# Hybrid decoder layer: first modulation rows loaded ahead of three pieces of the token-major x, idle matmuls behind the spread of the root mean square, row constants loaded later

## The chip, the cores and the metric

The kernel runs on one core of one Trainium2 chip. The metric is the device time of one execution in microseconds (us), smaller is better. Before the change the median of three runs is 734.33 us (732.56 to 735.61).

## The reference

One layer on x of 512 tokens by 2048 features, all float32:

```python
mod = silu(c) @ w_ada + b_ada                 # 3 * 2048
shift, scale, gate = split(mod, 3)
h = rms_norm(x) * (1.0 + scale) + shift
proj = h @ w_in                               # 4160 columns
xr, gr, qc, kvc, kr, ga = split(proj)
y_rnn = rg_lru_branch(xr, ...) * silu(gr)
y_att = mla_branch(qc, kvc, kr, positions, ...) * silu(ga)
x = x + gate * (concat([y_rnn, y_att]) @ w_out)
```

rms_norm divides each token by the root of the mean of its squares over the 2048 features, so it needs every feature of x before the first h can be made.

## The kernel before

**Layout.** Features lie on the 128 partitions and the 512 tokens along the free dimension: x, h and the projections are tiles of 128x512. The 2048 features are 16 tiles k. The projection goes over k in four chunks (`CHUNKS`: 2, 3, 4 and 7 tiles). Each product in float32 is made of three matmuls on split operands (high times high, high times low, low times high): ScalarE rounds the high part (`whi`, `wfs` half 0, `h`), VectorE subtracts for the low part (`wlo`, `wfs` half 1).

**The modulation.** Row j of the modulation is 128 values, the sums of w_ada times silu(c). `ada(j, parts)` (line 280) loads a 128x2048 piece of w_ada in the given parts (a part of 2 is 128x1024, 512 KB) and has VectorE multiply and sum each part (`ttr`, line 273; the operation stands in the profile as CUSTOM_DVE_ANT_0 at L276). `ada(16 + k)` gives the scale of tile k, `ada(k)` its shift. They share three buffers. `cb` holds silu(c) on every partition, made by eight matmuls and four copies.

**The start.** The token-major x (`xtok`) comes in eight pieces of 128x1024, 512 KB each (`xsq`, line 369; here called pieces 0 to 7). ScalarE squares and sums each one (`sqj`, sums in `ss8`). For every even piece TensorE transposes the first two feature tiles into `xps`, which ScalarE copies to `x0` and `x1`. Once all eight sums are there, VectorE and ScalarE make the inverse root mean square `rx` (lines 409 to 415), four matmuls spread it over the partitions (`rb_ps`, line 418), and VectorE makes tile 0: `x0` times scale and `rb_ps` (line 433), plus shift (line 442), the low part (line 445). Tile 1 follows with its own scale and shift. `proj_first` (line 497) then does the first eight column tiles with h0 (24 matmuls) and h1 (24 matmuls) and the weights `wfs`.

**Idle matmuls.** `warm(n, after)` (line 246) issues matmuls of a tile of ones (`junk`) into a bank that nobody reads: 4 at the start, 6 after each squared piece, 4 after the reciprocal, 14 behind the spread in program order. "After" is an order that is asked of the scheduler, not a wait on the chip.

**What sets the order.** SyncE's queue issues nearly all transfers in program order. The other engines' orders are set by a scheduler that simulates a timeline; each engine then runs its list in that order. `behind()` and `issue_after` tell it that an instruction may not stand before another. The vector constants (`vec`) and the first scale row `ada(16)` are loaded when the loop over the pieces reaches number `XA`, here 7. The row constants (`row`, a part for the attention's gains and one for its mask, and `pos_i`, the positions) are loaded behind the first weights (lines 463 to 465); VectorE scales and casts them as part of `setup_rope` (line 290).

```python
        if n == XA:
            DMA.dma_start(out=vec, in_=a["vec"])
            ts(vec[:, 16:32], vec[:, 16:32], 1.0, None, ALU.add)
            run(ada0[0])
        xsq(n // 2, n % 2)
```

Of the kernel before, what the change touches and what calls it, by code (L numbers as in the profile page):

```python
# [20 lines left out]
P = 128  # L21
# [17 lines left out]
NB0 = 0  # L39
NB1 = 1  # L40
P0 = 8
XA = 7
SETUP = (0, 2)
WARM = (4, 6, 4, 14)
NACC = 6
GRATE = 1.1
BANKS = dict(u=(0, 1), f=(2,), sc=(4, 5), tp=(6,), op=(6,), tq=(7,), oa=(2, 3, 0, 1, 7, 4, 5, 6))
# [4 lines left out]
R_QN, R_KN, R_QR, R_KR, R_IF, R_ID, R_MK, NROW = 0, 128, 256, 320, 384, 416, 544, 672  # L52
# [32 lines left out]
def body(ctx, nc, tc, a):  # L85
    V, G, A, PE, DMA = nc.vector, nc.gpsimd, nc.scalar, nc.tensor, nc.sync
    last_tab = [None]

    def act(out, in_, func, **kw):
        return A.activation(out=out, in_=in_, func=func, **kw)  # L90

    def tab(out, in_, func, **kw):
        if last_tab[0] is None:
            i = act(out, in_, func, **kw)
        else:
            with tc.issue_after(last_tab[0]):
                i = act(out, in_, func, **kw)
        last_tab[0] = i.ins if hasattr(i, "ins") else i
        return i

    def stt(out, in0, scalar, in1, op0, op1, **kw):
        return V.scalar_tensor_tensor(out=out, in0=in0, scalar=scalar, in1=in1, op0=op0, op1=op1, **kw)
# [6 lines left out]
    def ins_of(i):  # L109
        return i.ins if hasattr(i, "ins") else i  # L110

    def ts(o, i, s1, s2, o0, o1=None):
        if s2 is None:
            return V.tensor_scalar(out=o, in0=i, scalar1=s1, scalar2=None, op0=o0)
        return V.tensor_scalar(out=o, in0=i, scalar1=s1, scalar2=s2, op0=o0, op1=o1)
# [6 lines left out]
        return tt(lo, src, hi.bitcast(F32), ALU.subtract)  # L122

    def mm(out, lhsT, rhs, start, stop, **kw):
        PE.matmul(out=out, lhsT=lhsT, rhs=rhs, start=start, stop=stop, **kw)  # L125

    def mm3(out, wh, wl, xh, xl, start, stop, **kw):
        mm(out, wh, xh, start, False, **kw)
# [3 lines left out]
    def cols(i):  # L132
        return slice(i * P, (i + 1) * P)
# [14 lines left out]
    def run(gen):  # L148
        for _ in gen:
            pass  # L150
# [18 lines left out]
    def bank(kind, name):  # L169
        return psp.tile([P, S], F32, tag=f"b{next(cyc[kind])}", name=name)  # L170
# [6 lines left out]
    def bigt(n, name, dt=F32):  # L177
        return big.tile([P, 2, S], dt, tag=f"B{n}", name=name)
# [24 lines left out]
    row = cst.tile([P, NROW], F32, name="row")  # L203
    pos_i = cst.tile([P, NT], I32, name="pos_i")
    ident = row[:, R_ID:R_ID + P]
# [37 lines left out]
    def warm(n, after=None):  # L243
        with tc.issue_after(ins_of(after)) if after is not None else nullcontext():
            for _ in range(n):
                mm(junk_ps, junk[:, :P], junk, True, True)

    warm(WARM[0])
    cps = [bank("mm", "cb_ps") for _ in range(4)]
# [17 lines left out]
    def xload(k, keep=False):  # L267
        xt[k] = pjt(34 + k, F32, f"x{k}") if keep else xslot(f"x{k}")
        DMA.dma_start(out=xt[k], in_=a["x"][k])
# [4 lines left out]
    def ttr(t, cv, j, first, last):  # L274
        with behind():
            ttr_last[0] = V.tensor_tensor_reduce(  # L276
                out=t, in0=t, in1=cv, op0=ALU.mult, op1=ALU.add, scale=1.0,
                scalar=vec[:, C_BADA + j:C_BADA + j + 1] if first else modh[:, j:j + 1],
                accum_out=(mod if last else modh)[:, j:j + 1])

    def ada(j, parts=(4,)):
        t = p1.tile([P, 4, S], F32, tag="ada", name="ada", bufs=3)
        n0 = 0
        for w in parts:
            c = slice(n0, n0 + w)
            DMA.dma_start(out=t[:, c], in_=a["ada"][j][:, n0 * S:(n0 + w) * S].rearrange("p (k s) -> p k s", k=w))
            ttr(t[:, c], cb[:, c], j, n0 == 0, n0 + w == 4)
            n0 += w
            yield
# [79 lines left out]
    def xsq(i, j):  # L369
        t = bigt((2, 3, 8, 9, 10, 11, 12, 13)[2 * i + j], "xtok").rearrange("p k s -> p (k s)")  # L370
        DMA.dma_start(out=t, in_=a["xtok"][i][:, j * 1024:(j + 1) * 1024])
        sq = act(sqj, t, AF.Square, accum_out=ss8[:, j * 4 + i:j * 4 + i + 1])
        if j == 0:
            for k in range(KT0):
                PE.transpose(xps[k][:, i * P:(i + 1) * P], t[:, k * P:(k + 1) * P], ident)
        warm(WARM[1], sq)

    hh, hl = {}, {}
    ada0 = [ada(16, (2, 2)), ada(0, (2, 1, 1))]
    KT0 = CHUNKS[0][1]  # L380
    NG = NF // 4
    wfs = {(k, n): bigt(4 + k * NG + n, "wfs", F32R) for k in range(KT0) for n in range(NG)}
# [2 lines left out]
    def wf_load(k, n):  # L385
        raw = wfraw[k, n]
        DMA.dma_start(out=raw, in_=a["winf"][k, n])
        act(wfs[k, n][:, 0], raw, AF.Copy)

    def wf_lo(k, n):  # L390
        tt(wfs[k, n][:, 1], wfraw[k, n], wfs[k, n][:, 0].bitcast(F32), ALU.subtract)
# [3 lines left out]
    for n in range(2 * NT):  # L395
        if n == XA:
            DMA.dma_start(out=vec, in_=a["vec"])
            ts(vec[:, 16:32], vec[:, 16:32], 1.0, None, ALU.add)
            run(ada0[0])
        xsq(n // 2, n % 2)  # L400
    wf_load(0, 0)
    tab(p1.tile([P, 1], F32, name="sqrt0"), ones[:, 0:1], AF.Sqrt)
# [5 lines left out]
    vx, yx, tx, rx = (p1.tile([P, NT], F32, name=n) for n in ("vx", "yx", "tx", "rx"))  # L408
    tt(vx, ss8[:, 0:4], ss8[:, 4:8], ALU.add)
    ts(vx, vx, 1.0 / D, EPS, ALU.mult, ALU.add)  # L410
    warm(WARM[2], V.reciprocal(out=tx, in_=vx))
    tab(yx, tx, AF.Sqrt)
# [2 lines left out]
    mark[0] = ins_of(stt(rx, tx, 1.5, yx, ALU.add, ALU.mult))  # L415
    rb_ps = bank("aux", "rb_ps")
    for i in range(NT):
        mm(rb_ps[:, cols(i)], rx[:, i:i + 1].broadcast_to([P, P]), ident, True, True)
    rb = p1.tile([P, S], F32, tag="rb", name="rb")
    warm(WARM[3])  # L420

    def make_h(k):
        if k >= KT0:
            xload(k)
        parts = (2, 2) if k < KT0 else (4,)
        if k:
            yield from ada(16 + k, parts)
        x = xt[k]
        if k == 0:
            next(ada0[1])  # L430
            next(ada0[1])
            stt(x, x, mod[:, 16:17], rb_ps, ALU.mult, ALU.mult)
            act(rb, rb_ps, AF.Copy)
            yield from ada0[1]
        else:
            yield from ada(k, parts)
            stt(x, x, mod[:, 16 + k:17 + k], rb, ALU.mult, ALU.mult)
        t = bigt(k, f"h{k}", F32R)
        hh[k], hl[k] = t[:, 0], t[:, 1]
        if k < KT0:  # L440
            ts(hh[k], x, mod[:, k:k + 1], None, ALU.add)
        else:
            act(hh[k], x, AF.Identity, bias=mod[:, k:k + 1])
        i = stt(hl[k], x, mod[:, k:k + 1], hh[k].bitcast(F32), ALU.add, ALU.subtract)
        if k < KT0:
            mark[0] = ins_of(i)
# [12 lines left out]
    for n in range(NG):  # L459
        wf_load(1, n)  # L460
        with behind():
            wf_lo(1, n)
    DMA.dma_start(out=row[:, :R_ID], in_=a["row"][:, :R_ID])
    DMA.dma_start(out=row[:, R_MK:], in_=a["row"][:, R_MK:])
    DMA.dma_start(out=pos_i, in_=a["pos"])


    XR, GR, QC, KVC, GA, KR = 0, 8, 16, 20, 24, 32
# [34 lines left out]
    def proj_first(ms):  # L503
        k0, kc = CHUNKS[0]
        ps = [bank("mm" if n < 6 else "aux", "pp") for n, m in enumerate(ms)]
        for k in range(k0, k0 + kc):
            for i, (w, h) in enumerate(((0, hh), (0, hl), (1, hh))):
                for n, m in enumerate(ms):
                    mm(ps[n], wfs[k, n // 4][:, w, (n % 4) * P:(n % 4 + 1) * P], h[k], k == k0 and i == 0, k == k0 + kc - 1 and i == 2)
        for n, m in enumerate(ms):  # L510
            evac(0, m, ps[n])

    def proj_kr(ci):
        k0, kc = CHUNKS[ci]
        ps = bank("mm", "pk")
        raw = wraw()
        DMA.dma_start(out=raw[:, :kc * 64], in_=a[f"wkr{ci}"])
        hl_ = wtile("whi", "wkhl")
        w3 = hl_[:, :kc * P].rearrange("p (k h c) -> p k h c", k=kc, h=2)
        r3 = raw[:, :kc * 64].rearrange("p (k c) -> p k c", k=kc)  # L520
        act(w3[:, :, 0], r3, AF.Copy)
        tt(w3[:, :, 1], r3, w3[:, :, 0].bitcast(F32), ALU.subtract)
        for i, (h, l) in enumerate(hs(ci)):
            mm(ps, hl_[:, cols(i)], h, i == 0, False)
            mm(ps, hl_[:, cols(i)], l, False, i == kc - 1)
        evac(ci, KR, ps)

    LC = NCH - 1
    for ci in range(LC):
        nk0, nkc = CHUNKS[ci + 1]  # L530
        hgen = itertools.chain.from_iterable(make_h(k) for k in range(nk0, nk0 + nkc))
        done = 0
        ng = 32 // GROUP[ci]
        g0 = NF // GROUP[ci] if ci == 0 else 0
        if ci == 0:
            proj_first(MORDER[:NF])
        for g in range(g0, ng):
            while done < 2 * nkc * (g + 1 - g0) // (ng - 1 - g0):
                next(hgen, None)
                done += 1  # L540
            if g == (g0 + ng) // 2:
                proj_kr(ci)
            proj_group(ci, g)
        run(hgen)
    p1ctx.close()
    extra_raw[0] = False

# [641 lines left out]
```

## Time and profile before

| | |
|---|---|
| median of three runs | 734.33 us (732.56 to 735.61) |
| the profiled execution | 734.08 us |
| its span | 732.3 us |
| TensorE matmul busy | 720.5 us (98%) |
| TensorE weight load busy | 597.4 us (82%) |
| VectorE busy | 527.1 us (72%) |
| ScalarE busy | 353.6 us (48%) |
| mean granted TensorE clock | 0.995 of full |
| moved by the DMA engines | 127.94 MB, mean 175 GB/s |

Between the span and the time of the execution lie 1.8 us. A matmul's busy time in the profile includes its latency, so matmuls overlap and a busy TensorE need not be at its peak; the start-to-start pitch tells its pace. Group lists, waits and chains name an instruction by line, engine and tile; L125 is the helper that issues every matmul, L90 the one for ScalarE's activations, L118 that for differences on VectorE. "pp" is a projection's bank, "rb_ps" the spread root mean square, "wfs" the first weights, "PEclk" the clock that TensorE was granted as a share of 2.4 GHz.

### The profile page before, as it was taken

Reading aid. Unit: us, or ns where it says so; the run is one execution under the profiler, and the core shown is the slowest. Engines: PE = TensorE matmul, PEld = TensorE weight load, DVE = VectorE, ACT = ScalarE, POOL = GpSimd, SP = SyncE. Lnnn points to the kernel's source line nnn. Section 1 sums busy time; section 2 is a strip of 40 time slices with the busy share of each in tenths; the row PEclk is TensorE's granted clock in tenths of the full one; section 3 lists DMA queues with packets and bytes.
Section 4 is the critical chain, followed back from the end, with each engine's and each line's share of the span. In section 5 each row is a group of like instructions: output and inputs, shape, how many; then the busy total and the mean of one; then the engine's idle time right before and its main releaser. Section 6 shows DMA issues by size and latency. Waiting matters only on the chain.

```text
span 732.3 us, 10065 instructions
## 1 busy us (share of the span) xinstructions
PE 720.5 (98%) x3625; PEld 597.4 (82%) x3626; DVE 527.1 (72%) x949; ACT 353.6 (48%) x728; POOL 29.4 (4%) x34
## 2 busy tenths in 40 slices
PE   9799999999999999999999999999999999999998
PEld 4588887788888888878888888888888877888887
DVE  2997878899998889897765566567686677783232
ACT  7366322231223489875545568677465434222221
POOL 0000000000000000001011111111120100000000
PEclk9899999999999999999999999999999999999999
DMA  8998366987822322223243315213433799774330
GB/s 308 391 409 323 116 242 225 368 325 272 332 80 79 127 80 81 81 79 101 82 134 95 93 59 202 62 55 118 130 127 100 239 333 296 241 228 138 114 94 29
DMA packets 46002, 127.94 MB, mean 175 GB/s; under 512 B 5373, under 2 KB 9341, under 8 KB 42369
## 3 DMA queue, kind: packets, MB, share of 16 engines
q1 hardware_dynamic: 38896, 106.34, 42.1%
q10 hardware_dynamic: 7056, 20.97, 8.5%
q8 instruction: 28, 0.46, 0.2%
q14 instruction: 22, 0.17, 0.1%
HBM read 123.10 MB, written 4.19 MB: 174 GB/s over the span
## 4 chain that ended last, share of the span: by engine, by line
PE 79%; DMA 7%; DVE 5%; ACT 5%; issue 3%; SPq 1%; POOLq 0%; POOL 0%; ACTq 0%; DVEq 0%
PE pp L125 36%; PE oa L125 23%; PE sc L125 4%; PE uwqn L125 3%; PE uwuk L125 3%; DMA ada<-in_ada 3%; PE uwuv L125 3%; DMA xtok<-in_xtok 2%; PE op L125 2%; PE uqp L125 2%; DMA wraw<-in_wout 1%; PE tp L894 1%; ACT pj L90 1%; PE tq L794 1%; DVE xc L118 1%
## 5 line engine op out<-in xcount | busy, mean ns | idle before, releaser
L125 PE MATMUL pp<-h,whi 128*128 128x512 f32 x992 | 242.0, 391 | 0.5 <-ACT h L90 0.5
L90 ACT ACTIVATE whi<-wraw 128x512 fp32r<-128x512 f32 (+4 forms) x172 | 126.8, 740 | 207.5 <-PE pp L125 69.7
L125 PEld LDWEIGHTS pp<-h,whi 128*128 128x128 f32 x992 | 184.8, 188 | 39.7 <-ACT whi L90 1.0
L118 DVE TENSOR_TENSOR wlo<-wraw,whi 128x512 fp32r<-128x512 f32 (+4 forms) x172 | 141.0, 822 | 67.6 <-ACT whi L90 35.9
L125 PE MATMUL pp<-h,wlo 128*128 128x512 f32 x496 | 127.2, 390 | 1.5 <-DVE wlo L118 1.5
L125 PEld LDWEIGHTS pp<-h,wlo 128*128 128x128 f32 x496 | 92.7, 188 | 21.6 <-DVE wlo L118 2.5
L125 PE MATMUL oa<-yh,whi 128*128 128x512 f32 (+1 forms) x272 | 102.4, 384 | 0.1
L125 PE MATMUL oa<-yl,whi 128*128 128x512 f32 (+1 forms) x272 | 102.3, 380 | 0.0
L276 DVE CUSTOM_DVE_ANT_0 ada<-ada,cb,vec 128x2048 f32<-128x2048 f32 (+1 forms) x32 | 70.7, 2211 | 11.3 <-DMA ada<-in_ada 11.3
L118 DVE TENSOR_TENSOR pj<-pp,pj 128x512 f32<-128x512 f32 x96 | 64.0, 683 | 13.8 <-PE pp L125 13.2
L125 PE MATMUL oa<-yh,wlo 128*128 128x512 f32 (+1 forms) x272 | 71.8, 380 | 0.0
L125 PEld LDWEIGHTS oa<-yl,whi 128*128 128x128 f32 x272 | 51.3, 189 | 8.9 <-DVE yl L118 0.2
L125 PEld LDWEIGHTS oa<-yh,whi 128*128 128x128 f32 x272 | 51.3, 189 | 8.8 <-ACT yh L90 0.3
L125 PEld LDWEIGHTS oa<-yh,wlo 128*128 128x128 f32 x272 | 49.1, 188 | 9.1
L90 ACT ACTIVATE h<-x,mod 128x512 fp32r<-128x512 f32 x14 | 10.2, 730 | 33.4 <-DVE mod L276 17.7
L125 PE MATMUL sc<-kT,qT 128*128 128x128 f32 (+3 forms) x96 | 22.8, 332 | 1.1 <-ACT kT L90 1.1
L90 ACT ACTIVATE pj<-pp 128x512 f32<-128x512 f32 x32 | 17.4, 611 | 9.3 <-PE pp L125 9.3
L90 ACT ACTIVATE pr<-sc,nm 128x128 f32<-128x128 f32 (+3 forms) x32 | 16.7, 521 | 10.6 <-DVE nm L886 10.4
L276 DVE CUSTOM_DVE_ANT_0 ada<-ada,cbo,vec 128x1024 f32<-128x1024 f32 x16 | 20.5, 1279 | 1.2 <-DMA ada<-in_ada 1.2
L229 POOL TENSOR_TENSOR hs<-hs,mhalf 128x8 f32<-128x8 f32 x12 | 21.2, 1768 | 1.0
L276 DVE CUSTOM_DVE_ANT_0 ada<-ada,cbo,modh 128x1024 f32<-128x1024 f32 x16 | 20.5, 1279 | 0.9 <-DMA ada<-in_ada 0.9
L125 PE MATMUL uwuv<-whi,kvt 128*128 128x256 f32 x80 | 20.8, 284 | 0.0
(222 smaller groups left out, 1001.6 us busy)
## 6 DMA issues: line engine op xcount, KB each, us to landing
ada<-in_ada SPq DMA_DIRECT2D x28, 1024.0 KB, 7.9
ada<-in_ada ACTq DMA_DIRECT2D x32, 512.0 KB, 4.9
wraw<-in_wout SPq DMA_DIRECT2D x59, 256.0 KB, 3.6
wraw<-in_win SPq DMA_DIRECT2D x22, 512.0 KB, 6.5
wraw<-in_win SPq DMA_DIRECT2D x24, 448.0 KB, 3.2
wraw<-in_win SPq DMA_DIRECT2D x16, 384.0 KB, 4.2
xtok<-in_xtok SPq DMA_DIRECT2D x8, 512.0 KB, 7.3
xo<-in_x SPq DMA_DIRECT2D x16, 256.0 KB, 4.9
```

The source lines that it names most:

```text
L90: return A.activation(out=out, in_=in_, func=func, **kw)
L118: return V.tensor_tensor(out=o, in0=x, in1=y, op=op)
L125: PE.matmul(out=out, lhsT=lhsT, rhs=rhs, start=start, stop=stop, **kw)
L229: G.tensor_tensor(out=out, in0=out, in1=mhalf[:, :n], op=ALU.pow)
L276: ttr_last[0] = V.tensor_tensor_reduce(out=t, in0=t, in1=cv, op0=ALU.mult, op1=ALU.add, scale=1.0, scalar=vec[:, C_BADA + j:C_BADA + j + 1 ...
L794: PE.transpose(tp[:, d * 256 + i2 * P:d * 256 + (i2 + 1) * P], kt[u][:, q * P:(q + 1) * P], ident)
L894: PE.transpose(tp[:, j * P:(j + 1) * P], pr[:, j * P:(j + 1) * P], ident)
```

## The change

Four edits:

- `XA` goes from 7 to 5, and the first shift row `ada(0)` is run beside the first scale row `ada(16)`, in two parts where it had three. The vector constants and both rows (four transfers of 512 KB) are now issued ahead of pieces 5, 6 and 7; before, the constants and the scale row stood ahead of piece 7, and the shift row behind it.
- In `make_h(0)` the steps of the shift row are gone, since it is done before.
- The last idle matmuls go from 14 to 6 and are asked for behind the last of the four spreading matmuls.
- The row constants and positions are loaded after the first chunk's loop.

```diff
-XA = 7
+XA = 5
-WARM = (4, 6, 4, 14)
+WARM = (4, 6, 4, 6)
...
     def mm(out, lhsT, rhs, start, stop, **kw):
-        PE.matmul(out=out, lhsT=lhsT, rhs=rhs, start=start, stop=stop, **kw)
+        return PE.matmul(out=out, lhsT=lhsT, rhs=rhs, start=start, stop=stop, **kw)
...
-    ada0 = [ada(16, (2, 2)), ada(0, (2, 1, 1))]
+    ada0 = [ada(16, (2, 2)), ada(0, (2, 2))]
...
             run(ada0[0])
+            run(ada0[1])
         xsq(n // 2, n % 2)
...
     for i in range(NT):
-        mm(rb_ps[:, cols(i)], rx[:, i:i + 1].broadcast_to([P, P]), ident, True, True)
+        rbm = mm(rb_ps[:, cols(i)], rx[:, i:i + 1].broadcast_to([P, P]), ident, True, True)
...
-    warm(WARM[3])
+    warm(WARM[3], rbm)
...
         if k == 0:
-            next(ada0[1])
-            next(ada0[1])
             stt(x, x, mod[:, 16:17], rb_ps, ALU.mult, ALU.mult)
             act(rb, rb_ps, AF.Copy)
-            yield from ada0[1]
...
-    DMA.dma_start(out=row[:, :R_ID], in_=a["row"][:, :R_ID])
-    DMA.dma_start(out=row[:, R_MK:], in_=a["row"][:, R_MK:])
-    DMA.dma_start(out=pos_i, in_=a["pos"])
...
         run(hgen)
+        if ci == 0:
+            DMA.dma_start(out=row[:, :R_ID], in_=a["row"][:, :R_ID])
+            DMA.dma_start(out=row[:, R_MK:], in_=a["row"][:, R_MK:])
+            DMA.dma_start(out=pos_i, in_=a["pos"])
```

**SyncE's queue at the start.** It issues the transfers of the first 30 us; xtok are the pieces of the token-major x, ada the rows of the modulation, wfraw the first weights. Before:

```order
L371 DMA xtok<-in_xtok 128x1024 x7
L397 DMA vec<-in_vec 128x120
L286 DMA ada<-in_ada 128x1024 x2
L371 DMA xtok<-in_xtok 128x1024
L387 DMA wfraw<-in_winf 128x512
L286 DMA ada<-in_ada 128x1024
L286 DMA ada<-in_ada 128x512 x2
L387 DMA wfraw<-in_winf 128x512
L286 DMA ada<-in_ada 128x1024 x4
```

Now:

```order
L371 DMA xtok<-in_xtok 128x1024 x5
L397 DMA vec<-in_vec 128x120
L286 DMA ada<-in_ada 128x1024 x4
L371 DMA xtok<-in_xtok 128x1024 x3
L387 DMA wfraw<-in_winf 128x512 x2
L286 DMA ada<-in_ada 128x1024 x4
```

Ahead of the last piece of x stand four modulation transfers where there were two.

**ScalarE around the last squares.** sqj are the squares of the pieces, xps the transposed tiles, wfs the high parts of the first weights, yx the root. Before:

```order
L90 ACTIVATE sqj,ss_134<-xtok 128x1024 x2
L90 ACTIVATE spa<-vec 128x8
L90 ACTIVATE x_238<-xps 128x512
L90 ACTIVATE x_240<-xps 128x512
L90 ACTIVATE sqj,ss_134<-xtok 128x1024
L90 ACTIVATE wfs<-wfraw 128x512
L90 ACTIVATE yx<-tx 128x4
```

Now:

```order
L90 ACTIVATE sqj,ss_134<-xtok 128x1024 x2
L90 ACTIVATE x_243<-xps 128x512
L90 ACTIVATE x_245<-xps 128x512
L90 ACTIVATE sqj,ss_134<-xtok 128x1024
L90 ACTIVATE wfs<-wfraw 128x512 x2
L90 ACTIVATE yx<-tx 128x4
```

The copies of x0 and x1 still stand between the squares of pieces 6 and 7; a second weight copy now stands ahead of the root.

**TensorE around the spread.** In the list of before 22 pairs of idle matmuls stand between the last transposes (xps) and the spread (rb_ps); the end of it, the first projection's matmuls (pp) behind:

```order
L125 LDWEIGHTS junk
L125 MATMUL junk_ps<-junk 128x512
L125 MATMUL rb_ps<-row,rx 128x128 x4
L125 MATMUL pp<-h_286,wfs 128x512 x24
L125 MATMUL pp<-h_304,wfs 128x512 x24
```

Now (21 pairs stand ahead of the last transposes, 6 behind the spread, of which the first is shown):

```order
L125 LDWEIGHTS junk
L125 MATMUL junk_ps<-junk 128x512
L375 MATMUL xps<-row,xtok 128x128 x2
L125 MATMUL rb_ps<-row,rx 128x128 x4
L125 LDWEIGHTS junk
L125 MATMUL junk_ps<-junk 128x512
```

No idle matmul is left between the last transposes and the spread.

## Rows read from the trace of the kernel before

**Rows 1.** The page's busy time: engine, us, share of the span, instructions.

```profile
PE 720.5 (98%) x3625; PEld 597.4 (82%) x3626; DVE 527.1 (72%) x949; ACT 353.6 (48%) x728; POOL 29.4 (4%) x34
```

**Rows 2.** The chain that ended last, the start: start us, us, what.

```profile
9.35 10.56 DMA xtok<-in_xtok
...
26.57 30.36 PE pp L125 x120
```

**Rows 3.** Busy time by stretch: PE, PEld, DVE, ACT, POOL, granted clock, DMA share, GB/s.

```profile
22.30:25.70 3.40, 1.16 (x8) 0.97 (x8) 3.33 (x8) 1.06 (x2) 0.00 (x0) 1.00 1.03 411
25.70:26.00 0.30, 0.00 (x0) 0.00 (x0) 0.26 (x3) 0.17 (x1) 0.00 (x0) 0.55 0.99 396
26.00:32.00 6.00, 5.42 (x13) 4.29 (x14) 5.96 (x11) 1.26 (x2) 0.00 (x0) 0.50 1.04 390
...
32.50:32.70 0.20, 0.20 (x2) 0.15 (x2) 0.20 (x1) 0.00 (x0) 0.00 (x0) 0.86 1.00 410
```

**Rows 4.** The same view for TensorE alone: PE busy, granted clock, DMA share, GB/s.

```profile
26.57:34.86 8.29, 8.29 (x24) 0.64 1.03 383
...
40.45:45.89 5.44, 5.44 (x25) 1.00 1.00 412
```

**Rows 5.** SyncE's queue in order of time: start us, us, the transfer it issues.

```profile
13.29 0.33 SPq L286 DMA_DIRECT2D ada<-in_ada  x1
14.60 0.33 SPq L286 DMA_DIRECT2D ada<-in_ada  x1
```

**Rows 6.** ScalarE in order of time: start us, us, operation, [idle before, releaser].

```profile
13.36 1.06 ACT L90 ACTIVATE sqj<-xtok 128x1024 f32<-128x1024 f32 x1 [0.84 <-DMA xtok<-in_xtok]
...
16.54 1.06 ACT L90 ACTIVATE sqj<-xtok 128x1024 f32<-128x1024 f32 x1
...
17.70 1.06 ACT L90 ACTIVATE x<-xps 128x512 f32<-128x512 f32 x2
19.99 1.06 ACT L90 ACTIVATE sqj<-xtok 128x1024 f32<-128x1024 f32 x1 [1.23 <-DMA xtok<-in_xtok]
...
21.05 0.61 ACT L90 ACTIVATE wfs<-wfraw 128x512 fp32r<-128x512 f32 x1
21.79 0.20 ACT L90 ACTIVATE yx<-tx 128x4 f32<-128x4 f32 x1
```

**Rows 7.** VectorE in order of time.

```profile
17.52 1.28 DVE L276 CUSTOM_DVE_ANT_0 ada<-ada,cb,vec 128x1024 f32<-128x1024 f32 x1 [1.27 <-DMA ada<-in_ada]
...
21.17 0.16 DVE L118 TENSOR_TENSOR vx<-ss 128x4 f32<-128x4 f32 x1 [0.93 <-ACT sqj L90]
...
22.42 0.16 DVE L102 SCALAR_TENSOR_TENSOR rx<-tx,yx 128x4 f32<-128x4 f32 x1
...
24.49 0.74 DVE L102 SCALAR_TENSOR_TENSOR x<-x,mod,rb_ps 128x512 f32<-128x512 f32 x1
...
25.94 0.49 DVE L114 TENSOR_SCALAR h<-x,mod 128x512 fp32r<-128x512 f32 x1
...
33.82 0.32 DVE L114 TENSOR_SCALAR row<-row 128x128 f32<-128x128 f32 x2
...
34.27 0.48 DVE L114 TENSOR_SCALAR h<-x,mod 128x512 fp32r<-128x512 f32 x1
```

**Rows 8.** TensorE in order of time, idle matmuls, spread and first projection.

```profile
16.84 4.91 PE L125 MATMUL junk_ps<-junk 128*128 128x512 bf16 x22
...
22.63 1.16 PE L125 MATMUL rb_ps<-row,rx 128*128 128x128 f32 x8 [0.89 <-DVE rx L102]
```

**Rows 9.** SyncE, VectorE and TensorE around the later row constants.

```profile
48.01 2.37 SPq L196 DMA_DIRECT2D wraw<-in_win  x3
...
61.74 1.22 DVE L118 TENSOR_TENSOR wlo<-wraw,whi 128x1024 fp32r<-128x1024 f32 x1
...
65.97 1.52 PE L125 MATMUL pp<-h,wlo 128*128 128x512 f32 x6
```

**Rows 10.** TensorE's longest wait behind the first projection, 36 us to the end: us, times, longest.

```profile
PE pp L125 <- DVE wlo L118: 1.5, 2, 1.1
```

## The prediction

> **What bounds the kernel now.** I read the busy times first: TensorE has 720.5 of 732.3 us [rows 1]. Then its waits: behind the first projection the largest is 1.5 us in all [rows 10]. From about 27 us on TensorE is the bound, so what the change can move is the start: whatever it does to the moment at which TensorE is through with h0 and h1 shifts the rest of the program by as much, less what those few waits take up. The chain of waits says what the start hangs on: the transfer of piece 7 of x, 10.56 us from its issue at 9.35, then the root mean square, then h0, and from 26.57 matmuls without a break [rows 2].
>
> Two more views say what lies between. VectorE's order of time: rx ends at 22.58, tile 0's product with the spread starts at 24.49, its h0 at 25.94, and h1 runs from 34.27 to 34.75 [rows 7]; between h0 and h1 VectorE has no pause to speak of (5.96 us busy in 26 to 32 [rows 3]). The granted clock: full until 25.7, 0.55 in 25.7 to 26.0, half (1.2 GHz) from there, back to 2.4 GHz near 32.6 [rows 3]. The last idle matmul before had ended at 21.75 and the spread ran from 22.63 to 23.79 [rows 8], so the clock fell 4.0 us after the idle matmuls and came back 6.0 us after TensorE's restart at 26.57. That cost shows in the 24 matmuls of h0: 8.29 us, against 5.44 us for 24 at full clock [rows 4], a pitch of 0.227. With some 10 at that pitch in the last 2.3 us, 14 took 6.0 us, a pitch of 0.43. **But h1 was ready at 34.75, and h0's matmuls were over at 34.86.** The slow clock's 2.9 us were just hidden behind VectorE's way to h1. So it is h1's time that counts, and I follow that.
>
> **Piece 7 comes later (+2.6).** The queue brings 512 KB each 1.31 us: SyncE issues when an older transfer lands, at 13.29 (piece 4, which ScalarE squares at 13.36) and 14.60 [rows 5, 6]. Two more modulation transfers ahead of piece 7 make 2 x 1.3 = 2.6 us: it lands at 22.6 where it had landed at 19.9, piece 6 at 21.3. The vector constants and the scale row only move with them.
>
> **ScalarE gets in its way (+0.8, +0.5).** Between the squares of pieces 6 and 7 stand the copies of x0 and x1, 1.06 us [rows 6]. Before, piece 6 was squared at 16.54 and the copies fell into the wait for piece 7. Now pieces 6 and 7 land 1.3 us apart: square 21.3 to 22.4, copies to 23.4, so piece 7 is squared at 23.4 and not at 22.6; against 19.99 that is +3.4. A second weight copy of 0.61 us now stands ahead of the root yx: 23.4 + 1.06 + 2 x 0.6 = 25.7, where the root would have run at 21.79 + 3.4 = 25.2 [rows 6]. So rx ends at 22.58 + 3.9 = 26.5.
>
> **VectorE is freed (the gain).** The shift row's products, 1.28 us a half [rows 7], now run at about 17 to 21 us, where VectorE waits for ScalarE's sums anyway: nothing. Behind rx only spread, product and h0 are left. At full clock the spread takes 1.16 us [rows 8], at half up to twice that, 2.32; a gain it can't have. I take 2.1, close to twice, since TensorE will have been without idle matmuls for long: 21 idle matmuls follow piece 4's transposes, 4.9 us for 22 [rows 8], so they end near 18.5, and until 26.5 only one pair of transposes runs. That is 8.0 us where 4.0 were enough [rows 3, 8]. One could object that the transposes at 21.3 count as work, and that from 21.7 to 26.5 is 4.8 us, not far from 4.0. The Trainium skill, "TensorE: Matmul & The Clock Gate", Part 4 (PE-mode transpose), says that transposes don't count as busy for the clock. No run here shows that alone; by it the clock is low at the spread, and the sum is the one below; with the transposes counted and the clock held it would be 0.9 us less. So h0 starts 2.1 + 0.8 = 2.9 us behind rx where it started 3.4 behind, -0.5: at 29.4, +3.4. The way from h0 to h1 is the same list of VectorE work but for the casts and scalings of the row constants, 0.45 us from 33.82 to 34.27 [rows 7], which now come later: -0.45. **h1 is ready at 37.7, +3.0.**
>
> **TensorE's side.** Spread 26.5 to 28.6; six idle matmuls behind it at the half pitch, 6 x 0.43 = 2.6 us, to 31.2. h0 is ready at 29.9, so they hold the projection up by 1.3 us. If the clock comes back 6.0 us after this restart, at 32.5, three matmuls of h0 run slow and 21 at 0.227: over at 37.3, 0.5 before h1. So the idle matmuls and the clock cost nothing while that cover of 0.5 us lasts; gone, each us of low clock costs half a us. The eight idle matmuls taken out cost nothing either, nobody waits for them.
>
> **The row constants.** Their 128x416 and 128x128 floats are 272 KB, at 1.31 us for 512 KB 0.7 us of the queue ahead of tile 2's x and scale row, which nobody on TensorE waits for. Later they go in behind the first chunk's last weights, which went out with their successor in 48.0 to 50.4 [rows 9]; VectorE's casts now stand between the low parts of the fourth and fifth weight groups. The fifth was made at 61.74 to 62.96 and needed at 65.97 [rows 9]: 3 us of cover. If the constants land later than that, TensorE waits for the rest; I take nothing. On SyncE's queue one more thing moves: the second chunk's first shift row waits for the buffer of tile 1's scale row, which VectorE frees some 3 us later than before, and the next weights stand behind it. They are loaded two groups ahead of their matmuls, which cover it; without that cover it would be those 3 us once more, less the lead.
>
> **The sum.** 2.6 + 0.8 + 0.5 - 0.5 - 0.45 = +3.0 us on the profiled execution's 734.08: 737.1 us, its median of runs lying 0.25 above it. I take nothing off for TensorE's later waits, since those for low parts follow its own pace. The lower end of the unknowns: no collision on ScalarE (-1.3) and a spread at full clock (-0.9), +0.8.
>
> **The rivals.**
> 1. *The clock comes back too late (slower).* If the spread and the idle matmuls don't count and the 6.0 us run from the first projection matmul at 31.2, the clock is back at 37.2; 14 of the 48 matmuls are done by then, 34 x 0.227 = 7.7 take until 44.9, against 40.45 before: +4.5, 738.6. It decides from a return at 33.6 on. For it: before, six us of real matmuls were needed. Against it: the idle matmuls at the start kept the clock full.
> 2. *ScalarE is not in the way, or the clock holds.* +0.8 to +2.1: about 735.5. For it: before, piece 7's wait on ScalarE was 1.23 us [rows 6], so a little jitter in landings could let it by.
> 3. *The relief wins (faster).* If transfers did not land in order of issue and piece 7 came as before, only the gains would be left: 1.4 with a spread at full clock, 0.45 for the casts: -1.9, 732.2. Against it: each issue of SyncE follows the landing of the next older piece.
> 4. *The change doesn't do what it says.* The idle matmuls behind the spread are to bridge the gap, yet the order leaves none ahead of it. In the forecast this is so already; were the clock held in spite of it, h1 would still come 2.1 late, 736.2, which is in case 2.
>
> **How the numbers follow.** A measurement tells about 0.5% from no change, 3.7 us here, so 730.7 and 738.0 are the bounds. Forecast 0.42, of which 0.08 lies above 738.0; case 1 0.22; case 2 with 4 0.22; case 3 0.09; 0.05 for a gain that I don't see and that would go beyond 730.7. Slower 0.30, same 0.65, faster 0.05. The range leaves out case 3 and the far ends: 733.0 to 739.8.
>
> **What would show it.** Piece 7 squared near 23.4; rx at 26.5; TensorE at half clock when the spread starts; h0's first matmul near 31, h1's near 37.8; the casts of row constants near 60 us without a wait in front of a low part. I am wrong if piece 7 lands before 21.5, if the clock is full in 22 to 28, or if the low clock reaches into h1's matmuls.

## The result and the profile after

The change takes 736.31 us, the median of 20 runs (733.16 to 739.93), against 733.99 us for the kernel before, also of 20: a ratio of 1.0031 [1.0017, 1.0045], so 2.3 us more (1.2 to 3.3). 737.1 us was forecast. In the experiments below, one execution of 1207.7 us (load alone, second time) and one of 2553.1 us (idle matmuls and row constants without the load) stand far outside the others and are left out of the medians.

One thing has to be known before the profiles are read. The profiled execution of the change is the fastest of its 20: 733.16 us with a span of 731.4, while that of before, 734.08, lies near its median. The same kernel was profiled a second time later, and that execution has a span of 736.7 us. Put end against end, one of them would say that the change gains 0.9 us and the other that it costs 4.4. The first transfers do not arrive at the same time in every execution: ScalarE squares piece 4 at 13.36 us before [rows 6] and at 12.12 and 13.45 in the two of the change. Piece 4 is issued ahead of everything that the change moves, so below every time of the start is counted from its square.

The page of the change's first execution, busy time and granted clock, answers to [rows 1]:

```profile
PE 718.8 (98%) x3617; PEld 596.9 (82%) x3618; DVE 527.2 (72%) x947; ACT 353.6 (48%) x728; POOL 29.5 (4%) x34
...
PEclk9899999999999999999999999999999999999999
```

ScalarE in order of time, against [rows 6] (start, us, operation, idle before and who ended it):

```profile
12.12 1.06 ACT L90 ACTIVATE sqj<-xtok 128x1024 f32<-128x1024 f32 x1 [0.41 <-DMA xtok<-in_xtok]
...
18.70 1.06 ACT L90 ACTIVATE sqj<-xtok 128x1024 f32<-128x1024 f32 x1 [4.36 <-DMA xtok<-in_xtok]
...
19.98 1.06 ACT L90 ACTIVATE sqj<-xtok 128x1024 f32<-128x1024 f32 x1
...
21.04 1.06 ACT L90 ACTIVATE x<-xps 128x512 f32<-128x512 f32 x2
...
21.99 1.05 ACT L90 ACTIVATE sqj<-xtok 128x1024 f32<-128x1024 f32 x1
...
23.03 1.14 ACT L90 ACTIVATE wfs<-wfraw 128x512 fp32r<-128x512 f32 x2
...
24.07 0.20 ACT L90 ACTIVATE yx<-tx 128x4 f32<-128x4 f32 x1
```

Piece 5 now keeps ScalarE waiting 4.36 us, pieces 6 and 7 follow at the queue's own pace, and the two copies push the last square to 21.99, although its piece had landed at 21.19. The root yx, ready to run from 23.75 on, when VectorE's reciprocal ends, stands behind the second weight copy and runs at 24.07.

VectorE, against [rows 7]:

```profile
24.69 0.16 DVE L102 SCALAR_TENSOR_TENSOR rx<-tx,yx 128x4 f32<-128x4 f32 x1
...
27.02 0.75 DVE L102 SCALAR_TENSOR_TENSOR x<-x,mod,rb_ps 128x512 f32<-128x512 f32 x1 [2.17 <-PE rb_ps L125]
27.80 0.49 DVE L114 TENSOR_SCALAR h<-x,mod 128x512 fp32r<-128x512 f32 x1
...
35.80 0.49 DVE L114 TENSOR_SCALAR h<-x,mod 128x512 fp32r<-128x512 f32 x1
```

TensorE, against [rows 4, 8]:

```profile
14.86 4.48 PE L125 MATMUL junk_ps<-junk 128*128 128x512 bf16 x20
...
24.91 2.07 PE L125 MATMUL rb_ps<-row,rx 128*128 128x128 f32 x8 [4.53 <-DVE rx L102]
26.78 2.77 PE L125 MATMUL junk_ps<-junk 128*128 128x512 bf16 x6
28.98 6.71 PE L125 MATMUL pp<-h,wfs 128*128 128x512 f32 x24
36.44 5.68 PE L125 MATMUL pp<-h,wfs 128*128 128x512 f32 x24 [0.75 <-DVE h L114]
41.96 1.07 PE L125 MATMUL pp<-h,whi 128*128 128x512 f32 x4
```

The spread takes 2.07 us where it took 1.16. The projection of h0 is over at 35.69; TensorE then waits 0.75 us for h1. Before, the two had met within 0.1 us.

Busy time by stretch, against [rows 3] (the last three columns are granted clock, DMA share and GB/s):

```profile
20.00:22.00 2.00, 0.38 (x2) 0.14 (x2) 0.00 (x0) 2.00 (x5) 0.00 (x0) 1.00 1.05 397
22.00:24.00 2.00, 0.00 (x0) 0.00 (x0) 0.51 (x3) 2.00 (x5) 0.00 (x0) 1.00 1.03 408
24.00:26.00 2.00, 1.09 (x5) 1.09 (x6) 0.49 (x3) 0.27 (x2) 0.00 (x0) 0.51 1.03 411
...
28.00:30.00 2.00, 2.00 (x6) 1.20 (x5) 1.96 (x3) 1.62 (x3) 0.00 (x0) 0.50 1.08 425
30.00:32.00 2.00, 2.00 (x8) 1.59 (x8) 2.00 (x4) 0.00 (x0) 0.00 (x0) 0.78 0.95 391
32.00:34.00 2.00, 2.00 (x11) 1.64 (x10) 2.00 (x6) 0.00 (x0) 0.00 (x0) 1.00 0.28 100
```

The clock falls at about 24, before the spread, and is back at about 31, well ahead of h1's matmuls.

The second execution of the change, ScalarE's squares of pieces 4 and 7, VectorE's h1 and TensorE's matmuls behind it:

```profile
13.45 1.06 ACT L90 ACTIVATE sqj<-xtok 128x1024 f32<-128x1024 f32 x1 [0.62 <-DMA xtok<-in_xtok]
...
23.31 1.05 ACT L90 ACTIVATE sqj<-xtok 128x1024 f32<-128x1024 f32 x1
...
37.12 0.49 DVE L114 TENSOR_SCALAR h<-x,mod 128x512 fp32r<-128x512 f32 x1
37.76 5.73 PE L125 MATMUL pp<-h,wfs 128*128 128x512 f32 x24 [1.27 <-DVE h L114]
43.32 1.07 PE L125 MATMUL pp<-h,whi 128*128 128x512 f32 x4
```

Counted from piece 4's square, in us (the start of a row, or its start and length where something is made):

| | before | change, first | change, second | moved | forecast |
|---|---|---|---|---|---|
| piece 7 squared | 6.63 | 9.87 | 9.86 | +3.2 | +3.4 |
| rx made | 9.22 | 12.73 | 12.72 | +3.5 | +3.9 |
| h0 begun | 12.58 | 15.68 | 15.67 | +3.1 | +3.4 |
| h1 made | 21.39 | 24.17 | 24.16 | +2.8 | +3.0 |
| first matmul behind the first projection | 27.09 | 29.84 | 29.87 | +2.75 | |
| end of the span | 718.9 | 719.3 | 723.3 | +0.3, +4.3 | +3.0 |

Up to the end of the first projection the two executions agree to 0.03 us, and with the forecast to 0.4. Behind it they part by 4 us.

### The profile page after: what moved, and what is told of

Its sections match the earlier page's. It is cut to its first block, busy times and chain, and to the rows that moved or that the text cites. A ratio compares the mean times of both kernels' runs of the same rounds, so it can differ in the third digit from the quotient of the medians.

```text
span 731.4 us, 10041 instructions
## 1 busy us (share of the span) xinstructions
PE 718.8 (98%) x3617; PEld 596.9 (82%) x3618; DVE 527.2 (72%) x947; ACT 353.6 (48%) x728; POOL 29.5 (4%) x34
## 4 chain that ended last, share of the span: by engine, by line
PE 78%; DMA 7%; DVE 6%; ACT 5%; issue 3%; SPq 1%; ACTq 0%; DVEq 0%
PE pp L125 35%; PE oa L125 23%; PE sc L125 3%; PE uwqn L125 3%; PE uwuk L125 3%; DMA ada<-in_ada 3%; PE uwuv L125 3%; DMA xtok<-in_xtok 2%; PE op L125 2%; DMA wraw<-in_wout 2%; PE uqp L125 2%; DVE ada L276 1%; PE tp L893 1%; ACT pj L90 1%; PE tq L793 1%
## 5 line engine op out<-in xcount | busy, mean ns | idle before, releaser
L118 DVE TENSOR_TENSOR pj<-pp,pj 128x512 f32<-128x512 f32 x96 | 64.0, 683 | 14.0 <-PE pp L125 13.5
L125 PE MATMUL uwqn<-whi,kvt 128*128 128x256 f32 x80 | 20.7, 286 | 0.0
```

Of the source, the lines that this page charges most:

```text
L118: return V.tensor_tensor(out=o, in0=x, in1=y, op=op)
L125: return PE.matmul(out=out, lhsT=lhsT, rhs=rhs, start=start, stop=stop, **kw)
```

## The experiments

The places of the table serve for every run: "the block" is the first matmul behind the first projection, counted from piece 4's square, against 27.09 before. Times are medians with the ratio to the kernel before on the same chip.

**The change profiled again** (no edit).

> The changed kernel beside its parts on one chip: 1.2 to 3.3 us above before, as it was; first block's end 2.7 us later than before, counted from the square of piece 4.

Measured: 736.54 us, 1.0027 [1.0008, 1.0046]. Its start was shown above. Where do the 4 us come from? The waits of TensorE from 100 to 260 us, first execution and second:

```profile
PE pp L125 <- ACT h L90: 0.5, 1, 0.5
```

```profile
PE pp L125 <- DVE wlo L118: 2.7, 2, 1.6
PE pp L125 <- ACT h L90: 0.5, 1, 0.5
```

VectorE and TensorE around the larger of the two new waits, second execution:

```profile
186.74 2.35 DVE L276 CUSTOM_DVE_ANT_0 ada<-ada,cb,vec 128x2048 f32<-128x2048 f32 x1 [2.12 <-DMA ada<-in_ada]
...
190.28 1.22 DVE L118 TENSOR_TENSOR wlo<-wraw,whi 128x1024 fp32r<-128x1024 f32 x1
...
191.55 2.12 PE L125 MATMUL pp<-h,wlo 128*128 128x512 f32 x8 [1.61 <-DVE wlo L118]
```

and VectorE at the same place in the first:

```profile
181.83 2.35 DVE L276 CUSTOM_DVE_ANT_0 ada<-ada,cb,vec 128x2048 f32<-128x2048 f32 x1 [0.54 <-DMA ada<-in_ada]
```

A modulation row that lands later holds VectorE 1.6 us longer; the low part of the weights stands behind it, and TensorE waits 1.61 us where it waited for nothing. Counted from piece 4's square, the two executions are 1.9 us apart just ahead of this wait and 3.6 behind it; the rest comes behind 500 us. Why the rows land later in one execution was not found.

**The load alone**: `XA = 5`, `ada(0, (2, 2))` run beside the scale row, its steps out of `make_h(0)`; idle matmuls and row constants as before. It was run twice.

```diff
-XA = 7
+XA = 5
...
-    ada0 = [ada(16, (2, 2)), ada(0, (2, 1, 1))]
+    ada0 = [ada(16, (2, 2)), ada(0, (2, 2))]
...
             run(ada0[0])
+            run(ada0[1])
...
```

> The kernel before with the load order alone (both first modulation rows ahead of pieces 5 to 7, none in the way of tile 0); idle matmuls and row constants as before. Way to h1 (mine): piece 7 lands 2.6 us later, two weight copies and the two copies of x stand between its square and the root, so rx comes about 4 later, h1 about 3.5 later: slower by 2 to 4 us, 737. Idle matmuls as the cause: with 35 idle matmuls ahead of the spread the clock holds, so it would be faster than the whole change, at or below the kernel before. Row constants as the cause: no change against before.

> The load order alone once more, beside the whole change on one chip. By the way to h1 it should be 0.7 us slower than the whole change, since its root waits longer on ScalarE; if the idle matmuls or the late row constants add something of their own to the whole change, it is faster than that by 1 us or more, as the first look suggested.

Measured: 734.46 us, 1.0004 [0.9988, 1.0019], and 735.33 us, 1.0012 [0.9994, 1.0030]. The block came 3.5 and 3.4 us later, so the start does what the terms say, and more than in the whole change. The spread took 2.08 and 1.85 us, so the 35 idle matmuls ahead of it did not hold the clock; the rival, by which they would, missed. Yet the time hardly moved: the expectation of the time missed. At 106 us the two executions are still 3.5 and 3.4 late, at 185 us 1.6 and 1.7. In between TensorE waits less than before [rows 10]: the same waits view of 100 to 260 us has no entry here, where before it has two:

```profile
PE pp L125 <- ACT h L90: 0.5, 1, 0.5
PE pp L125 <- DVE wlo L118: 0.4, 1, 0.4
```

What matmuls in 100 to 195 us start later than the pitch of 0.227 after one another sums to 0.15 and 0.43 us, before to 1.95 us. The scheduler's list for the later chunks is another one in this kernel, beyond the moved instructions. Which difference removes the waits was not tried.

**The idle matmuls alone**: 6 behind the spread, in place of 14.

```diff
-WARM = (4, 6, 4, 14)
+WARM = (4, 6, 4, 6)
...
-    warm(WARM[3])
+    warm(WARM[3], rbm)
...
```

> The kernel before with the idle-matmul edit alone (6 behind the spread, 8 left ahead of it). Way to h1 (mine): h1 stays where it was, some 12.2 us behind rx; whatever the clock does in h0's 24 matmuls, the time is within 0.5 us of before. Clock (rival): the slow clock of before cost the end 2.9 us, and a clock that is back sooner gives up to that: 731 to 732.

Measured: 734.64 us, 1.0006 [0.9989, 1.0022]. In this execution the clock never fell, as the windows show:

```profile
18.00:22.00 4.00, 2.03 (x11) 0.83 (x10) 2.59 (x9) 2.95 (x6) 0.00 (x0) 1.00 1.04 401
22.00:26.00 4.00, 2.37 (x15) 1.43 (x15) 3.85 (x9) 1.23 (x2) 0.00 (x0) 1.00 1.03 410
26.00:30.00 4.00, 4.00 (x18) 3.29 (x18) 4.00 (x7) 1.10 (x2) 0.00 (x0) 1.00 1.05 384
```

and TensorE's second half of the projection waits for h1 all the same:

```profile
34.15 2.08 PE L125 MATMUL pp<-h,wfs 128*128 128x512 f32 x8 [1.60 <-DVE h L114]
```

The block moved by 0.1 us. A full clock throughout the first projection is worth nothing here, because h1 is what it waits for.

**The row constants alone**: the three transfers moved behind the first chunk's loop.

```diff
-    DMA.dma_start(out=row[:, :R_ID], in_=a["row"][:, :R_ID])
...
         run(hgen)
+        if ci == 0:
+            DMA.dma_start(out=row[:, :R_ID], in_=a["row"][:, :R_ID])
...
```

> The kernel before with the later row constants alone. Way to h1 (mine): h1 0.45 us earlier, but TensorE is still busy with h0 at the slow clock until about 34.9 us, so nothing to 0.4 us faster. Row constants as the cause of the loss (rival): VectorE waits for their landing in front of the fifth weight group's low part, and the time is 1 to 3 us above before.

Measured: 733.29 us, 0.9989 [0.9975, 1.0004]; the block 0.33 us earlier. The casts between h0 and h1 had been put at 0.45. Nothing on the slower side comes from this part.

**The change with XA = 7**: two rows still go ahead of piece 7, but pieces 5 and 6 come early, so the copies of x0 and x1 lie in the wait for piece 7 again.

```diff
-XA = 5
+XA = 7
```

> The changed kernel with the modulation rows moved back to stand ahead of piece 7 alone (XA 7). Piece 7 lands as late as in the change, but pieces 5 and 6 are squared before, so the copies of x0 and x1 fall into the wait. Way to h1 (mine): rx 0.8 us or a little more earlier than in the change, h1 likewise; time 0.5 to 1 us below the change, still 1 us or more above before. Rival (the collision on ScalarE is nothing): same as the change.

Measured: 734.11 us, 0.9994 [0.9979, 1.0009]. ScalarE's copies and the last square:

```profile
17.69 1.09 ACT L90 ACTIVATE x<-xps 128x512 f32<-128x512 f32 x2 [1.09 <-PE xps L375]
...
21.33 1.06 ACT L90 ACTIVATE sqj<-xtok 128x1024 f32<-128x1024 f32 x1 [2.56 <-DMA xtok<-in_xtok]
```

Piece 4 was squared at 12.16, so the last square is 9.17 behind it, 2.5 more than before and 0.7 less than in the change: the collision, put at 0.8. The block came 2.1 us late instead of 2.75. In the median nothing is left of those 2.1 us (0.7 at most by its interval), where 1 us or more had been expected to stay, while this execution's span still ends 1.65 late; what takes them up behind the start was not found.

**ScalarE freed**: in the change, the copies of x0 and x1 asked for behind piece 7's square, the weight copies behind the root.

```diff
-        xsq(n // 2, n % 2)
-    wf_load(0, 0)
+        sq7 = xsq(n // 2, n % 2)
...
-        act(xt[k], xps[k], AF.Copy)
+        with tc.issue_after(ins_of(sq7)):
+            act(xt[k], xps[k], AF.Copy)
...
+    with tc.issue_after(ins_of(yxi)):
+        wf_load(0, 0)
...
```

> The changed kernel with the copies of x0 and x1 behind piece 7's square and the first weight copies behind the root on ScalarE. Way to h1 (mine): piece 7 is squared when it lands, 0.8 us earlier; the root gains 0.2 more; rx and h1 come 1.0 us earlier, the time falls by 0.5 to 1.0 us. Rival (the landing alone counts): the time of the change.

Measured: 734.65 us, 1.0004 [0.9985, 1.0023]; the block 2.0 us late, 0.75 less than in the change. The last square came 9.16 behind piece 4's, as with XA = 7. The copies of x0 and x1 now stood ahead of the root where a weight copy had stood, so that second term was not taken away.

**The clock held**: in the change, 20 idle matmuls between the last transposes and the spread.

```diff
+    warm(20, xtr[0])
     for i in range(NT):
-        rbm = mm(rb_ps[:, cols(i)], ...
+        with tc.issue_after(ins_of(wlastmm[0])):
+            rbm = mm(rb_ps[:, cols(i)], ...
```

> The changed kernel with 20 more idle matmuls between the last transposes and the spread, so that TensorE has no pause ahead of it. Way to h1 (mine): the clock is full at the spread, which takes 1.16 us and not 2.07; h1 comes 0.9 us earlier; the time falls by 0.4 to 0.9 us against the change. Clock (rival): the first projection's slow clock is what costs, and 2 us or more come back, down to or below the kernel before.

Measured: 735.07 us, 1.0011 [0.9992, 1.0029]. It did not do what it was to do:

```profile
21.11 6.17 PE L125 MATMUL junk_ps<-junk 128*128 128x512 bf16 x20
27.11 1.05 PE L125 MATMUL rb_ps<-row,rx 128*128 128x128 f32 x8
...
29.62 4.82 PE L125 MATMUL pp<-h,wfs 128*128 128x512 f32 x20 [0.16 <-ACT rb L90]
```

```profile
20.00:22.00 2.00, 1.17 (x6) 0.68 (x7) 0.00 (x0) 1.88 (x5) 0.00 (x0) 0.95 1.05 405
22.00:24.00 2.00, 2.00 (x6) 0.75 (x5) 0.00 (x0) 2.00 (x6) 0.00 (x0) 0.50 1.03 408
```

The clock fell just as the idle matmuls began, so most of them ran at half speed, and the spread stood behind the last of them at 27.11 although rx was made at 25.74. Block +3.1. What it does show: with the clock full from 26 us on, h0's matmuls and h1's all ran at full speed, and the block was no earlier, since the late spread had put h1 0.3 us later than in the change.

**Idle matmuls and row constants without the load.**

```diff
-WARM = (4, 6, 4, 14)
+WARM = (4, 6, 4, 6)
...
+        if ci == 0:
+            DMA.dma_start(out=row[:, :R_ID], in_=a["row"][:, :R_ID])
...
```

> The kernel before with the idle-matmul edit and the later row constants, load order as before. Way to h1 (mine): h1 0.45 us earlier and TensorE through with h0 before that, so 0.2 to 0.5 us faster than before. Clock (rival): 2 us or more faster.

Measured: 733.59 us, 0.9989 [0.9967, 1.0010]; the block 0.2 us earlier. Both parts without the load cost nothing, so the late start comes with the load. The change was not run with one of these two parts taken out, so what they might cost together with the load is open.

**The same, with the low parts of h0's weights on GpSimd** in place of VectorE.

```diff
-        tt(wfs[k, n][:, 1], wfraw[k, n], wfs[k, n][:, 0].bitcast(F32), ALU.subtract)
+        e = G if k == 0 else V
+        e.tensor_tensor(out=wfs[k, n][:, 1], ...
```

> As the one before, and the low parts of h0's first weights made on GpSimd, which takes 1.4 us of VectorE's work out of the way to h1. Way to h1 (mine): h1 1.8 us earlier than before, TensorE then the bound at 33.4 to 34: 1 to 1.5 us faster than before, if GpSimd is done by 32 us. Rival (h1's time does not set the end): no change against the one before it.

Measured: 734.20 us, 0.9998 [0.9982, 1.0014]; the block 0.1 us later, not earlier. GpSimd and VectorE just ahead of the spread:

```profile
21.30 1.26 POOL L392 TENSOR_TENSOR wfs<-wfraw,wfs 128x512 fp32r<-128x512 f32 x1 [20.88 <-ACT wfs L90]
...
21.59 0.99 DVE L118 TENSOR_TENSOR tx<-yx 128x4 f32<-128x4 f32 x1 [0.27 <-ACT yx L90]
```

A product of four elements a partition, 0.16 us in the change's own trace, took 0.99 on VectorE and ended 0.02 us behind GpSimd's subtraction. rx came 0.8 us late by it, and h1 no earlier than with the idle matmuls and row constants alone.

**A dose**: the kernel before, with four and with eight more 256 KB transfers ahead of piece 7, into tiles that nothing reads yet.

```diff
         if n == XA:
+            for i in range(4):
+                DMA.dma_start(out=pjt(i, F32, f"pad{i}"), in_=a["x"][i])
```

> The kernel before with 1 MB of x loaded once more ahead of the first scale row and piece 7, into tiles that nobody reads: a pure delay of 2.6 us in the way to h0 and h1. All of it passes through (as I predicted): the first chunk's first block ends 2.6 us later and the time is 2.3 to 2.6 us above before. Part is taken up later (what the traces of the late-starting kernels hint at, 1.2 to 2 us between 40 and 167 us): the block 2.6 later, the time 0.5 to 1.5 above before.

> The same with 2 MB: a delay of 5.2 us. All passes through: 5 us above before. Part is taken up: the taking-up is a fixed amount of 1.2 to 2 us, then 3.2 to 4 above before; if it is a share, 1 to 3.

Measured: with four 737.25 us, 1.0050 [1.0027, 1.0072], 3.7 us more (2.0 to 5.3); with eight 741.08 us, 1.0087 [1.0052, 1.0121], 6.4 us more (3.8 to 8.9). Piece 4 and piece 7 on ScalarE with four:

```profile
11.91 1.06 ACT L90 ACTIVATE sqj<-xtok 128x1024 f32<-128x1024 f32 x1 [0.73 <-DMA xtok<-in_xtok]
...
21.25 1.06 ACT L90 ACTIVATE sqj<-xtok 128x1024 f32<-128x1024 f32 x1 [2.61 <-DMA xtok<-in_xtok]
```

That is 9.34 against 6.63, +2.7; the block +2.8. With eight, piece 7 came 6.6 us later, where 5.2 had been expected, and the block 6.75; why it is more than twice the 2.7 was not found. The lists of the engines are the kernel's own but for a few neighbours that change places. A late block thus passes into the time whole by the medians; the intervals leave room for 0.8 and 2.9 us of it to be taken up by later waits, as had been thought possible. The padded transfers also put later what follows on SyncE's queue (the first weight behind piece 7 lands 2.7 us later, counted from piece 4's square), while in the change tile 1's first row lands when it did before (11.7 us behind that square against 11.8). So they are not the change's late start alone.

## Why the prediction was right, point by point

**Piece 7 +2.6.** Shown: pieces 4 and 7 land 9.15 us apart (12.04 and 21.19) instead of 6.64, +2.5. Transfers landed in order of issue, so the rival in which the relief wins fell.

**ScalarE's collision, +0.8 and +0.5.** The first part is shown by its own removal: with XA = 7 the last square is 0.7 us earlier. The second measured 0.3 (from piece 7's square to rx 2.86 us, before 2.59). So the rival without the collision fell too.

**VectorE's relief.** The spread at half clock took 2.07 us (2.1 was taken; at full clock before, 1.16), and h0 starts 2.95 behind rx where it had 3.36: 0.4, forecast 0.5. From h0's start to h1's end the way is 0.3 us shorter, forecast 0.45; the row constants moved alone gave the same 0.3.

**TensorE's clock.** The clock was at 1.00 in 22 to 24 us and at 0.51 in 24 to 26; since the last idle matmuls ended at 19.34, only a pair of transposes had run. The Trainium skill, "TensorE: Matmul & The Clock Gate", Part 4, has transposes not count as busy; by that rule the clock falls, and the trace agrees, as far as one pair can tell. Counted from piece 4's square it was back after some 18.8 us, 19.1 were forecast, and h0's matmuls were over 0.6 us before h1 was made, 0.5 were forecast. The rival in which the clock comes back too late fell: no slow matmul reached h1, and with the clock full throughout, the idle matmuls alone gave nothing. Nor was the clock held in spite of the pause, the way left to the rival in which the change does not do what it says.

**The signs of being wrong.** One came up to the letter: in the first execution piece 7 landed at 21.19, before 21.5. That bound belongs to a start in which piece 4 landed at 13.27 us; here it landed at 12.04, and in the second execution, where piece 4 landed at 13.37, piece 7 landed at 22.50. The clock was not full through 22 to 28, and it was back before h1's matmuls.

**The row constants later: nothing.** The scaling stands at 60 us between two low parts, as said, and TensorE has no wait there. VectorE in the change:

```profile
59.17 1.23 DVE L118 TENSOR_TENSOR wlo<-wraw,whi 128x1024 fp32r<-128x1024 f32 x1 [0.46 <-ACT whi L90]
60.31 0.32 DVE L114 TENSOR_SCALAR row<-row 128x128 f32<-128x128 f32 x2
```

**The sum.** h1 was made 2.8 us late, 3.0 were forecast, and the time rose by 2.3 (1.2 to 3.3). Each of the five terms was one or two tenths too large, those of either sign. Up to h1 the forecast is right by its mechanism.

**The step that did not hold** is the last of the sum: "I take nothing off for TensorE's later waits, since those for low parts follow its own pace." Up to 106 us it holds: in each of the 14 profiled executions the delay of the block is still there, to 0.15 us, in the matmuls around that time, so the weights that stand behind the shift row's buffer cost nothing either. Between 107 and 187 us it does not hold. There the first execution of the change gave back 1.2 us of its 2.75 and the second lost another 2.3; behind 500 us they gave back 1.2 and 0.7. The waits there do not only follow TensorE, they follow transfers that land early or late: the same kernel had 0.5 us of them in one execution and 3.2 in another. They may also follow the list that the scheduler makes anew for each kernel; that was not shown.

With the load alone these waits were gone, and 3.5 us at the start were worth 0.3 and 0.9 us at the end. With XA = 7, with ScalarE freed and with the idle matmuls ahead of the spread the block was 2 to 3 us late too, and the medians rose by 0.8 us at most. So what lies behind the block gave 1.7 to 3.2 us back in those kernels and 0.5 us in the change, by medians whose intervals reach 1.0 to 1.4 us either way; only XA = 7, at most 0.7 us above before, lies clear of the change, at least 1.2 above it. That the time of the change came within 0.8 us of the forecast is therefore in part luck: the forecast had no reason why this kernel gives so little back. Why it does stays open. No run held the later lists fixed and moved the start alone; the padded transfers come nearest, and those passed the delay on whole by the medians.

No kernel here beats the one before by more than its interval: the two fastest medians, the row constants alone and idle matmuls with row constants, are 0.9 and 0.75 us under, with intervals that hold 1.

## What to carry to other kernels

Follow the instruction that the block waits for last, here h1, and not the loss that is easiest to see: in the kernel before, 7 us of half clock cost nothing while h1 was later still, and in the change only the spread's 0.9 us of them lay on the way to h1 (2.07 against 1.16; no run had the change's start with a full clock at a spread on time). A transfer that is moved ahead of a critical one costs its whole time on the queue, and earlier VectorE work repays it only as far as that work had been on the critical path. Compare single profiled executions by a marker ahead of the change; end against end the same kernel differed here by 5 us, more than the change is worth.

## What the runs showed of the hardware that had not been expected

- A GpSimd instruction can hold up one of VectorE's. While GpSimd subtracted for 1.26 us, VectorE's product of two operands, four elements a partition, took 0.99 us instead of 0.16. The Trainium skill, "SBUF — State Buffer", section "Who interferes with whom", says that a VectorE instruction with two inputs in SBUF contends with a GpSimd instruction that reads SBUF, and that the one issued second blocks until the first is through. The trace agrees: it ended 0.02 us behind GpSimd's.
- The same list at the start kept the clock in one execution and not in another. With the idle matmuls alone TensorE went without matmuls from 19.8 to 21.8 us and the clock stayed at 1.00 (shown above). With the row constants moved as well, its list at the start is the same, but it went without them from 18.9 to 21.7, and the clock fell:

```profile
22.00:26.00 4.00, 3.54 (x15) 1.64 (x14) 3.84 (x9) 1.23 (x2) 0.00 (x0) 0.60 1.03 410
```

  The spread starts within 0.1 us of the same time in both; the pause begins 0.9 us earlier in the second. That goes back to the 22 idle matmuls which open TensorE's list, the idle matmuls alone first, both parts second:

```profile
1.59 7.80 PE L125 MATMUL junk_ps<-junk 128*128 128x512 bf16 x22 [1.59 <-DVE spe L355]
```

```profile
1.59 6.95 PE L125 MATMUL junk_ps<-junk 128*128 128x512 bf16 x22 [1.59 <-DVE spe L355]
```

  Behind them TensorE works its list without a wait up to the pause. That the longer pause is what lost the clock was not tried.

- Piece 4 was squared between 11.9 and 13.5 us in the 14 profiled executions, with the same transfers ahead of it; the span of one execution can move by as much from that alone.
